# Hybrid encoder, layer 1: one instruction list from the last down projections of layer 0 to the output projection

## The chip, the cores and the metric

The kernel runs on one core of a Trainium2 chip. TensorE does the matmuls, VectorE and ScalarE the elementwise work, GpSimd some elementwise work, and SyncE (SP) issues the DMAs. The metric is the device time of one execution in microseconds; below 0.2% two versions are not told apart here.

## What is computed

A two-layer encoder over two sequences (16 meta tokens and 256 tokens; 16 and 512), with shared weights and in float32. Layer 0 has latent attention, layer 1 windowed attention with a sink per head; both have a squared-ReLU MLP, and the norm stands behind each addition.

```python
for i in range(DEPTH):
    mix = mla_mixer(h, ...) if i % 2 == 0 else gqa_mixer(h, ...)
    h = layer_norm(DN_ALPHA * h + mix, ln1_g[i], ln1_b[i])
    h = layer_norm(DN_ALPHA * h + sqrelu_mlp(h, mlp_w1[i], mlp_w2[i]), ln2_g[i], ln2_b[i])

def gqa_mixer(x, cos, sin, w_qkv, sink, w_o):     # layer 1
    q, k, v = split(x @ w_qkv)                     # 16 query heads, 4 key/value heads of 64
    q, k = partial_rope(q), partial_rope(k)        # the first 16 columns of a head turn
    # a block of 128 queries sees the 16 meta keys and the keys within 128 positions
    s = where(mask, q k^T / 8, -1e30);  m = max(max(s), sink)
    p = exp(s - m) / (sum(exp(s - m)) + exp(sink - m))
    return (p v) @ w_o
```

## The kernel before

Activations lie with the 1024 features on partitions (8 blocks of 128) and the 800 tokens in two halves of 400 columns (`hf` 0 and 1). A product in float32 is made of three matmuls of split operands (`mm3`, L417): high times high, high times low, low times high. So each operand is made as a pair: a cast on ScalarE gives the high part, a subtraction on VectorE the low part (`split`, L434; for weights L297 and L298 in `Weights.load`, which also issues the DMA on SP; three raw and three split buffers, `wraw` and `wsp`).

The two MLPs (`mlp_middle`, L1001) are written as a list of tasks for a `Plan` (L97). A task names its engine, a cost, what it reads and writes, and the buffers it holds. `Plan.order` lays the tasks out in time by these costs, with TensorE's tasks in the order in which they were written, and a buffer free again when the last task that holds it is done (`left`). `Plan.issue` writes all engines' instructions in that order, under `tc.manual_schedule`. The MLP's list ends with the splits of three down weights for the stage after it (`ahead`, L1508 to L1513).

Everything between the two lists is left to the scheduler of the tile framework, which orders each engine's instructions by its own estimate, with hints (`tc.high_priority`, `tc.issue_after`, `after`):

- the last group of down projections of layer 0 (`down0`, L1529), first half, then second, each followed by a layer norm (`ln_fm`, L459): a matmul for the mean, subtractions, squares, sums, a matmul for the sums, square root and reciprocal, a matmul to spread it, then per block a multiplication on VectorE, a scaling on ScalarE (L481) and the split;
- the query, key and value projections (`qk_chunk`, L1601, with the rotation on VectorE and GpSimd; values from L1632). `half_first` (L968) starts with the first half of six chunks and loads three weights twice;
- the attention: 24 items, four pairs of query chunks (`cp`) times six blocks (`b`). `scores1` (L1669) makes two sets of six score matmuls, two row halves of the array at a time, 272 columns wide (400 in blocks 3 and 4), with the masked maximum on VectorE (L1688). `soft` does the exponentials on ScalarE, `norm` the scaling on VectorE and GpSimd (L1725, L1727). `av1` (L1732) transposes the probabilities (L1747 meta, L1756) and multiplies by the values (L1765, L1770). The pieces of five neighbouring items are issued in turns by `GQA_ORDER` (L52), transposes three items behind their scores;
- the output projection (L1809 to L1824), first half, layer norm, second half. Then layer 1's `mlp_middle` begins; its sixth matmul is followed by the mean of the second half (L1147).

PSUM is divided anew for each of these stages (`psum_phase`).

Of the kernel before, what the change touches and what calls it, by code (L numbers as in the profile page):

```python
# [46 lines left out]
QN = 3  # L47
QKV_FIRST = [("q", c) for c in range(2, 2 + QN)] + [("q", 0), ("q", 1), ("k", 0)] + [("q", c) for c in range(2, 2 + QN)]
QKV_REST = [("k", 1)] + [("q", c) for c in range(2 + QN, 8)] + [("v", 0), ("v", 1)]


GQA_ORDER = [("s", 0, 0), ("a", 0, 3), ("a", 1, 3), ("s", 3, 1), ("a", -1, 4), ("s", 1, 0), ("a", 2, 3), ("a", 3, 3), ("s", 2, 0)]  # L52

GQA_LOADS = (4, 5, 6)
GQA_LAG = max(lag for _, _, lag in GQA_ORDER)

# [5 lines left out]


FILL = (None, "pm", "pm", "st", "rb", "rb")
DOWN_FILL = (None, "pm", "pm", "pm", "pm", "pm", "st", "rb")
DOWN_ADD = (None, None, "va", "va", "va", "va", "va", "va")
DOWN_LOAD = ("va", "va", "rc")
# [22 lines left out]
class Held:  # L90


    def __init__(self, tag, make, t=None):
        self.tag, self.make, self.t, self.left, self.fresh = tag, make, t, 0, True


class Plan:  # L97
# [5 lines left out]

    def __init__(self, bufs, own):
# [11 lines left out]
    def task(self, engine, cost, run, reads=(), writes=(), new=(), port=False):  # L116
# [143 lines left out]
    def issue(self):  # L260
        order = self.order()
        tiles = {tag: [make(k) for k in range(self.bufs[tag] - len(self.given[tag]))] for tag, make in self.own.items()}
        for i in order:
            _, _, run, _, held, _ = self.tasks[i]
            for h in held:
                if h.t is None:
                    if h.tag in self.own:
                        k = self.at[id(h)]
                        h.t = tiles[h.tag][k] if isinstance(k, int) else k
                    else:  # L270
                        h.t = h.make()
            run()


class Weights:
# [9 lines left out]
    def load(self, parts=1):  # L285
# [20 lines left out]
        return True  # L306

# [22 lines left out]
def tile_encoder(ctx: ExitStack, tc: tile.TileContext, ins: dict, y):  # L330
# [72 lines left out]
    for layer in range(2):  # L403
        w1 = ins[f"w1_{layer}"]
        if layer == 1:
            for e in QKV_FIRST + QKV_REST:
                use(e, ins["w_" + e[0]][e[1]])
            for _ in range(2):
                for o in range(8):
                    use(("o1", o), ins["w_o1"][o])  # L410
        for j in UP_FIRST[:2]:
            use(("up", j), w1[j])
        for i in range(4):
# [1585 lines left out]
```

## Time and profile before

| | us |
|---|---|
| median of three runs | 1839.02 (1835.86 to 1839.11) |
| the profiled execution | 1837.13 |
| its span | 1835.3 |
| TensorE busy in the span | 1789.3 (97%) |
| VectorE, ScalarE, GpSimd busy | 1351.6, 1011.4, 783.9 |

The span runs from the first instruction to the last on the slowest engine. A matmul's time in the profile includes its way through the array and overlaps the next one, so durations are no measure of TensorE's speed; from start to start is. A busy TensorE can still be slow. The granted clock is given as a share of 2.4 GHz; its two levels are 1.0 and 0.5.

### The profile page before, as it was taken

To read this page: it belongs to the slowest core of one execution; us is meant where nothing else is said; L and a number is where in the kernel's file an instruction comes from. 1 tells how busy PE (TensorE), PEld (TensorE's weight loads), DVE (VectorE), ACT (ScalarE), POOL (GpSimd) and SP (SyncE) were. 2 spreads that over 40 slices of the span, in tenths; PEclk is the share of its full clock that TensorE was granted. 3 is DMA by queue.
4 is the path that set the end of the run, shared out by engine and by line. 5 is a ranking of instruction groups with operands and counts; after the bars stand their busy time and mean duration, and the time that the engine had idled before them with its cause. 6 is when DMAs were issued, how large, how long until landed. Compare 5 with 4: busy or idle time off the path is not lost.

```text
span 1835.3 us, 28950 instructions
## 1 busy us (share of the span) xinstructions
PE 1789.3 (97%) x10808; PEld 1645.0 (90%) x10808; DVE 1351.6 (74%) x2552; ACT 1011.4 (55%) x2146; POOL 783.9 (43%) x616
## 2 busy tenths in 40 slices
PE   9989999999999999999999999999999999999997
PEld 9989889979999999999999997569989889888896
DVE  5478778775876887788776867774875887778767
ACT  5357766773655445544553526782674455545642
POOL 0046655662245445545522232331333566456623
PEclk9999999999999999999999999999999999999999
DMA  5110001104311211222131221002211211222122
GB/s 194 47 41 31 18 21 33 38 29 140 109 58 47 82 59 61 76 71 68 58 122 58 70 73 54 2 1 88 97 63 64 71 67 49 92 69 69 47 92 92
DMA packets 37868, 120.12 MB, mean 65 GB/s; under 512 B 4576, under 2 KB 8800, under 8 KB 37600
## 3 DMA queue, kind: packets, MB, share of 16 engines
q1 hardware_dynamic: 37728, 118.28, 19.3%
q8 instruction: 85, 1.39, 0.3%
q14 instruction: 55, 0.45, 0.1%
HBM read 115.12 MB, written 3.15 MB: 64 GB/s over the span
## 4 chain that ended last, share of the span: by engine, by line
PE 70%; DVE 19%; ACT 6%; issue 3%; POOL 2%; DMA 1%; DVEq 0%; ACTq 0%; POOLq 0%; SPq 0%
PE w L418 14%; PE w L420 14%; PE w L419 14%; PE o L420 2%; PE o L419 2%; PE o L418 2%; PE s L1680 2%; DVE wsp0d L1064 2%; DVE wsp L298 2%; DVE h L1106 2%; PE in L418 1%; PE in L419 1%; PE in L420 1%; PE gav L1765 1%; DVE acc L1371 1%
## 5 line engine op out<-in xcount | busy, mean ns | idle before, releaser
L721 POOL TENSOR_SCALAR p<-p,rs 106x512 f32<-106x512 f32 (+3 forms) x128 | 184.4, 1450 | 134.8 <-DVE pk L720 63.7
L1371 DVE TENSOR_TENSOR acc<-acc,w 128x400 f32<-128x400 f32 (+1 forms) x306 | 176.9, 616 | 21.1 <-PE w L420 18.8
L1106 DVE TENSOR_TENSOR h<-sq,h 128x384 fp32r<-128x384 f32 (+1 forms) x165 | 142.7, 880 | 26.7 <-ACT h L1104 26.6
L297 ACT CAST wsp<-wraw 128x1024 fp32r<-128x1024 f32 (+2 forms) x85 | 78.2, 928 | 78.5 <-PE o L420 62.1
L298 DVE TENSOR_TENSOR wsp<-wraw,wsp 128x1024 fp32r<-128x1024 f32 (+2 forms) x85 | 102.0, 1206 | 21.3 <-ACT wsp L297 20.9
L418 PE MATMUL w<-h,wsp0d 128*128 128x400 f32 x336 | 116.2, 346 | 1.1 <-DVE acc L1371 1.0
L420 PE MATMUL w<-h,wsp0d 128*128 128x400 f32 x336 | 115.7, 344 | 0.3 <-DVE wsp0d L1064 0.3
L419 PE MATMUL w<-h,wsp0d 128*128 128x400 f32 x336 | 116.0, 345 | 0.0
L418 PE MATMUL w<-wsp1d,h 128*128 128x512 f32 x252 | 100.0, 397 | 5.6 <-DVE acc L1371 5.6
L1112 POOL TENSOR_TENSOR sq<-sq,sq 128x400 f32<-128x400 f32 (+1 forms) x56 | 75.1, 1342 | 70.2 <-DVE h L1106 58.1
L420 PE MATMUL w<-wsp1d,h 128*128 128x512 f32 x252 | 100.2, 398 | 0.3
L419 PE MATMUL w<-wsp1d,h 128*128 128x512 f32 x252 | 99.7, 396 | 0.0
L1104 ACT CAST h<-sq 128x384 fp32r<-128x384 f32 (+1 forms) x165 | 84.3, 518 | 26.2 <-POOL sq L1112 24.4
L419 PE MATMUL o<-o,wsp 128*128 128x400 f32 (+1 forms) x256 | 87.9, 343 | 1.3 <-DVE o L435 1.3
L420 PE MATMUL o<-o,wsp 128*128 128x400 f32 (+1 forms) x256 | 87.9, 343 | 1.4 <-DVE wsp L298 1.4
L418 PE MATMUL o<-o,wsp 128*128 128x400 f32 (+1 forms) x256 | 88.8, 347 | 0.3 <-ACT o L435 0.3
L1077 POOL TENSOR_TENSOR wraw0d<-wraw0d,wraw0d 128x512 f32<-128x512 f32 x48 | 69.8, 1472 | 41.2 <-DMA wraw0d<-in_w2b_dram 29.3
L745 ACT ACTIVATE p<-s,nm,rq 106x528 f32<-106x528 f32 (+1 forms) x80 | 63.4, 794 | 41.0 <-DVE nm L744 32.3
L1285 DVE TENSOR_TENSOR sq<-sq,w 128x400 f32<-128x400 f32 (+1 forms) x69 | 38.6, 560 | 52.9 <-PE w L420 52.7
L1058 ACT CAST wsp0d<-wraw0d 128x1024 fp32r<-128x1024 f32 x42 | 43.2, 1050 | 57.6 <-POOL wraw0d L1077 46.1
L743 DVE TENSOR_REDUCE nm<-s 106x1 f32<-106x528 f32 (+1 forms) x80 | 55.8, 700 | 18.3 <-PE s L420 17.4
L1064 DVE TENSOR_TENSOR wsp0d<-wraw0d,wsp0d 128x1024 fp32r<-128x1024 f32 x42 | 63.5, 1512 | 7.1 <-ACT wsp0d L1058 7.1
(1379 smaller groups left out, 6275.7 us busy)
## 6 DMA issues: line engine op xcount, KB each, us to landing
wraw<-in_w_o_dram SPq DMA_DIRECT2D x32, 512.0 KB, 3.3
wraw0d<-in_w2b_dram SPq DMA_DIRECT2D x24, 512.0 KB, 3.2
wraw1d<-in_w2b_dram SPq DMA_DIRECT2D x18, 512.0 KB, 4.0
wraw<-in_w_q_dram SPq DMA_DIRECT2D x11, 512.0 KB, 3.6
wraw<-in_w_in_dram SPq DMA_DIRECT2D x6, 512.0 KB, 4.1
wraw<-in_w_qn_dram SPq DMA_DIRECT2D x8, 384.0 KB, 3.0
wx1d<-in_w2b_dram SPq DMA_DIRECT2D x6, 512.0 KB, 3.2
out_dram<-acc SPq DMA_DIRECT2D x12, 256.0 KB, 2.0
```

What stands on the lines that cost most here:

```text
L297: nc.scalar.copy(sp[:, 0, a:b], raw[:, a:b])
L298: nc.vector.tensor_tensor(sp[:, 1, a:b], raw[:, a:b], sp.bitcast(F32)[:, 0, a:b], ALU.subtract)
L418: nc.tensor.matmul(out, lh, rh, start=start, stop=False, **kw)
L419: nc.tensor.matmul(out, lh, rl, start=False, stop=False, **kw)
L420: nc.tensor.matmul(out, ll, rh, start=False, stop=stop, **kw)
L721: G.tensor_scalar(pt[:qm, META:T], pt[:qm, META:T], rs[:qm, h : h + 1], None, ALU.mult)
L1064: lambda: V.tensor_tensor(dst.t[:, 1, dc], src.t[:, sc], dst.t.bitcast(F32)[:, 0, dc], ALU.subtract),
L1077: lambda x=x, y=y, z=z: G.tensor_tensor(x[0].t[:, x[1]], y[0].t[:, y[1]], z[0].t[:, z[1]], op),
L1104: plan.task("ACT", 530, lambda: S.copy(d.t[:, 0], c.t[:, :n]), reads=[c], writes=[(d, "hi")], new=[d])
L1106: "DVE", 570, lambda: V.tensor_tensor(d.t[:, 1], c.t[:, :n], d.t.bitcast(F32)[:, 0], ALU.subtract),
L1112: plan.task("POOL", 185 + 1.67 * n, lambda: G.tensor_tensor(out.t[:, :n], x.t[:, :n], y.t[:, :n], op), reads=[x, y], writes=[out])
L1371: f = lambda: V.tensor_tensor(z, z, ps.t[:, : z.shape[-1]], ALU.add)
```

## The change

The part between the two MLPs becomes a third `Plan`, `attention1`, with its own list of tasks and TensorE's order written out: the eight down projections of the first half, eight of the second with the first half's norm between them; then query chunks 0 and 1, values, and the other chunks of the first half; chunks 4 to 7 and both key chunks for both halves; then the attention by blocks (blocks 0 to 2 of all pairs, block 5, blocks 3 and 4), with steps of two blocks of k of other projections (`fill`) put between scores, transposes and outputs: the second half of the values and of chunks 0 to 3, and, when blocks 0 to 2 are through, the first half of the output projection. Six weights are loaded twice (four query chunks, two of values). A set of six scores, the transposes of four tiles and a block's value products are one task each. The attention's output takes the place of the queries. `stage` is a task-less buffer that opens memory pools when the tasks that use the old ones are done. `issue(behind)` puts the first instruction of a list on each engine behind the last one of the list before. PSUM stays one ring of eight banks. In `mlp_middle` the three down weights made ahead count as held to the end (`w.left += 1`).

The core of the diff (the bodies of the norm, of the softmax and of the output projection do the same operations as before):

```diff
+FIRST_Q = 4
+ITEMS = [(cp, b) for b in range(3) for cp in range(4)] + [(cp, 5) for cp in range(4)] + [(cp, b) for cp in range(4) for b in (3, 4)]
+BEHIND_T, BEHIND_A = 2, 1
+BESIDE = (3000, 2000, 2000, 1600, 2200, 2200, 2200)
...
+    def stage(self, tag, make):
+        h = Held(tag, make)
+        self.bufs[tag] = 1
+        self.given[tag], self.turns[tag] = [], [h]
+        h.after = set()
+        return h
...
+            deps.update(h.after)
+        for h in ends:
+            h.after.add(n)
...
+            f = getattr(run(), "ins", None)
+            if f is not None:
+                if behind is not None and e in first:
+                    behind(f, first.pop(e))
+                last[e] = f
...
             ahead.append(w)
+            w.left += 1
-            plan.issue()
+            plan.issue(after if l else None)
...
-    psum_phase(w=6, l=2)
-    W.places["last"] = W.places[None]
...
+        plan = Plan(
+            {"wsp": 3, "wraw": 3, "wh": 1, "w": 8, "sqb": 6, "ssb": 1, "ssc": 1, "sqc": 6, "rt": 2, "sh": 1, "sma": 4, "smb": 3, "pta": 2, "ptb": 2,
+             "rm": 4, "nm": 4, "rs": 4, "es": 4, "pk": 4, "ptm": 2, "mask": 1},
...
+        plan.busy = {"DVE": 700.0, "ACT": 700.0, "POOL": 300.0}
+        DVE, ACT, POOL = lambda n: 150 + 1.05 * n, lambda n: 170 + 0.835 * n, lambda n: 185 + 1.67 * n
+        MM = {400: 183, 384: 174, 256: 119}
+        both = lambda *names: [(x, y) for x in names for y in ("hi", "lo")]
+        st1 = plan.stage("projections", open_projections)
+        st2 = plan.stage("attention", open_attention)
+        st3 = plan.stage("wide", open_wide)
+        st4 = plan.stage("norm", open_norm)
...
+        def down(hf, o, between=None):
+            w, ps, a0 = wd[o // 2], new("w"), o % 2 * P
+            def run():
+                for k in range(4):
+                    t, a = tiles[LAST + k][hf], k * 256 + a0
+                    mm3(ps.t[:, :HALF], w.t[:, 0, a : a + P], w.t[:, 1, a : a + P], t[:, 0], t[:, 1], k == 0, k == 3)
+            plan.task("PE", 12 * MM[HALF], run, reads=[w, *both(w)], writes=[ps], new=[ps], ends=[st1])
+            z = acc[:, hf]
+            plan.task("DVE", DVE(HALF), lambda: V.tensor_tensor(z[:, o], z[:, o], ps.t[:, :HALF], ALU.add), reads=[ps], writes=[("acc", hf, o)])
...
+        mean0, sums0, scale0 = layer_norm("b0", 0, acc[:, 0], HALF, 2, 3, lambda: ssb[0].t, out_b(0), "H", "sqb", [ssb[0]], [st2])
+        mean1, sums1, scale1 = layer_norm("b1", 1, acc[:, 1], HALF, 2, 3, lambda: ssb[1].t, out_b(1), "H", "sqb", [ssb[1]], [st2])
...
+            def step(ks):
+                def run():
+                    for k in ks:
+                        a = k * P
+                        mm3(ps.t[:, :n], w.t[:, 0, a : a + P], w.t[:, 1, a : a + P], H[hf][0][:, k, c0:], H[hf][1][:, k, c0:], k == 0, k == 7)
+                plan.task("PE", 6 * MM[n], run, reads=[w, *both(w, *[("H", hf, k) for k in ks])], writes=[ps], new=[ps] if ks[0] == 0 else [], ends=end)
+                if ks[-1] < 7:
...
+                def run(ci=ci, ps=ps):
+                    Q, K = at["Q"][cp], at["K"]
+                    for x, (i, j) in enumerate(((0, 0), (0, 1), (1, 0))):
+                        for gi in range(2):
+                            rows = slice(64 * gi, 64 * gi + 64)
+                            nc.tensor.matmul(ps[gi].t[:, :w], Q[rows, i, ci, q0 : q0 + P], K[j][rows, gp2, k0 : k0 + w], start=x == 0, stop=x == 2)
+                reads = both(("q", 2 * cp + ci, hf), *[("k", gp2, x) for x in kh])
+                plan.task("PE", 3 * (120 if w == 272 else 181) + 100 * (1 - ci), run, reads=[st1, *reads], writes=ps, new=ps, ends=[st4])
...
+        after0 = {0: mean0, 4: sums0, 6: scale0}
+        for o in range(8):
+            down(0, o)
+        for o in range(8):
+            down(1, o)
+            if o in after0:
+                after0[o]()
+        for c in range(2):
+            w = wq(c)
+            for i, f in enumerate(rope("q", c, 0, w)):
+                f()
+                if (c, i) == (0, 3):
+                    mean1()
+        wv = [weights(ins["w_v"][i], f"v{i}") for i in range(2)]
+        for f in values(0, wv):
+            f()
+        for c in range(2, 8):
+            w = wq(c)
+            for i, f in enumerate(rope("q", c, 0, w)):
+                f()
+                if (c, i) == (2, 0):
+                    sums1()
+                if (c, i) == (2, 2):
+                    scale1()
+            if c >= FIRST_Q:
+                for f in rope("q", c, 1, w):
+                    f()
+        for c in range(2):
+            w = weights(ins["w_k"][c], f"k{c}")
+            for hf in range(2):
+                for f in rope("k", c, hf, w):
+                    f()
+        plan.task("SP", 3700, lambda: nc.sync.dma_start(mask.t, ins["mask"][:, MASK_OFF[1] :]), reads=[st2], writes=[mask], new=[mask])
...
+        def fill():
+            wv = [weights(ins["w_v"][i], f"v{i}b") for i in range(2)]
+            for f in values(1, wv):
+                yield 24 * MM[256], f
+            for c in range(FIRST_Q):
+                w = wq(c, "b")
+                for f in rope("q", c, 1, w):
+                    yield 6 * MM[HALF], f
+            yield 0, None
+            for o in range(8):
+                w = weights(ins["w_o1"][o], f"o0{o}")
+                for f in project(0, o, w):
+                    yield 6 * MM[NH], f
...
+        def some(upto):
+            nonlocal done, through
+            while done < upto and not (through and n < 12 + behind):
+                cost, f = next(steps)
+                done += cost
+                if f is None:
+                    through = True
                 else:
+                    f()
+        for n in range(len(ITEMS) + behind):
+            if n < len(ITEMS):
+                cp, b = ITEMS[n]
+                while not {("q", 2 * cp + i, b // 3) for i in range(2)} <= made:
+                    some(done + 1)
+                soft[n] = scores(*ITEMS[n])
+            time += BESIDE[min(n // 4, len(BESIDE) - 1)]
+            some(time - BESIDE[0] / 2)
+            if 0 <= n - BEHIND_T < len(ITEMS):
+                turned[n - BEHIND_T] = transposes(*ITEMS[n - BEHIND_T], *soft.pop(n - BEHIND_T))
+            some(time)
+            if n == 12 + behind - 1:
+                time = done
+            if 0 <= n - behind < len(ITEMS):
+                outputs(*ITEMS[n - behind], *turned.pop(n - behind))
+        for _, f in steps:
+            f()
+        mean2, sums2, scale2 = layer_norm("c0", 0, acc[:, 0, :, META:], NH, 4, 5, lambda: ssc.t[:, :NH], lambda o: (at["h"][0][:, 0, o], at["h"][1][:, 0, o]), ...
+        after1 = {(0, 3): mean2, (2, 2): sums2, (3, 0): scale2}
         for o in range(8):
+            w = weights(ins["w_o1"][o], f"o1{o}")
+            for i, f in enumerate(project(1, o, w)):
+                f()
+                if (o, i) in after1:
+                    after1[o, i]()
+        ahead = [weights(ins["w1_1"][j], f"up{j}") for j in UP_FIRST[:2]]
+        for w in ahead:
+            w.left += 1
+        with tc.manual_schedule(engines={mybir.EngineType.PE, mybir.EngineType.DVE, mybir.EngineType.Activation, mybir.EngineType.Pool, mybir.EngineType.SP}):
+            plan.issue(after)
```

## Rows read from the trace of the kernel before

**Rows 1.** The page: its span, TensorE's busy time, one row of its DMA issues.

```profile
span 1835.3 us, 28950 instructions
...
PE 1789.3 (97%) x10808; PEld 1645.0 (90%) x10808; DVE 1351.6 (74%) x2552; ACT 1011.4 (55%) x2146; POOL 783.9 (43%) x616
...
wraw<-in_w_q_dram SPq DMA_DIRECT2D x11, 512.0 KB, 3.6
```

**Rows 2.** Sums by stretch; columns: stretch, length, busy time of each engine, granted clock, DMA.

```profile
1001.40:1020.90 19.50, 18.16 (x91) 16.59 (x89) 17.03 (x34) 13.12 (x25) 3.19 (x3) 0.91 0.09 28
1120.80:1246.65 125.85, 122.71 (x882) 75.03 (x881) 96.29 (x387) 101.47 (x331) 37.64 (x53) 0.99 0.06 20
1246.65:1317.50 70.85, 70.85 (x406) 70.58 (x405) 45.29 (x58) 28.81 (x40) 17.26 (x13) 1.00 0.32 105
1317.50:1330.60 13.10, 10.84 (x51) 9.89 (x51) 12.28 (x22) 7.73 (x15) 2.19 (x3) 0.87 0.21 80
```

**Rows 3.** TensorE in order of time, end of layer 0's MLP: start, us, what, idle before.

```profile
956.63 0.34 PE L418 MATMUL w<-h,wsp_30z 128*128 128x400 f32 x1
...
958.65 0.34 PE L420 MATMUL w<-h,wsp_30z 128*128 128x400 f32 x1
961.87 0.46 PE L418 MATMUL w<-h,w 128*128 128x400 f32 x1 [2.88 <-DVE sq L1285]
...
965.38 0.54 PE L418 MATMUL dn<-h,wsp0c 128*128 128x400 f32 x1
```

**Rows 4.** VectorE in order of time, at the same place.

```profile
960.11 1.23 DVE L1064 TENSOR_TENSOR wsp0c<-wraw0c,wsp0c 128x1024 fp32r<-128x1024 f32 x1 [0.97 <-ACT wsp0c L1058]
961.25 0.56 DVE L1285 TENSOR_TENSOR sq<-sq,w 128x400 f32<-128x400 f32 x1
```

**Rows 5.** ScalarE in order of time, first layer norm: scalings of two neighbouring blocks.

```profile
1004.81 0.72 ACT L481 ACTIVATE acc<-acc,gb 128x400 f32<-128x400 f32 x1
...
1005.99 0.72 ACT L481 ACTIVATE acc<-acc,gb 128x400 f32<-128x400 f32 x1
```

**Rows 6.** TensorE in order of time, attention: whole pieces, and broken sets of scores.

```profile
1169.41 1.01 PE L1680 MATMUL s<-k,q 64*128 64x272 f32 x12
1170.36 1.08 PE L1765 MATMUL gav<-pt,v 128*64 128x256 f32 x8
...
1186.27 0.45 PE L1680 MATMUL s<-k,q 64*128 64x400 f32 x1
1186.65 1.08 PE L1765 MATMUL gav<-pt,v 128*64 128x256 f32 x6
...
1189.04 0.81 PE L1680 MATMUL s<-k,q 64*128 64x400 f32 x5
1189.78 0.66 PE L1756 MATMUL gt<-ident,sm 128*128 128x128 f32 x4
...
1240.03 1.09 PE L1756 MATMUL gt<-ident,sm 128*128 128x128 f32 x8
1240.96 0.38 PE L1747 MATMUL gm<-ident,pk 128*64 128x128 f32 x2
1241.18 0.60 PE L1756 MATMUL gt<-ident,sm 128*128 128x128 f32 x4
1241.71 1.51 PE L1765 MATMUL gav<-pt,v 128*64 128x256 f32 x12
1243.15 0.65 PE L1770 MATMUL gav<-ptm,vm 64*64 64x256 f32 x4
1243.73 0.66 PE L1756 MATMUL gt<-ident,sm 128*128 128x128 f32 x4
```

**Rows 7.** TensorE and VectorE in order of time, first mean of layer 1's MLP.

```profile
1320.98 1.57 PE L1147 MATMUL w<-sqsum,part 128*128 128x400 f32 x2 [2.26 <-DVE sqsum L1824]
...
1320.28 0.56 DVE L1824 TENSOR_TENSOR sqsum<-sqsum,acc 128x400 f32<-128x400 f32 x1
```

**Rows 8.** VectorE in order of time, attention: a masked maximum behind GpSimd.

```profile
1203.41 0.44 DVE L1688 CUSTOM_DVE_ANT_0 sm<-s,mask 128x272 f32<-128x272 f32 x1 [0.84 <-POOL sm L1725]
```

More of the change, by code (lines that the diff above doesn't have):

```diff
@@ L93, in __init__ @@
     def __init__(self, tag, make, t=None):
[L94 removed]
+        self.tag, self.make, self.t, self.left, self.fresh, self.after = tag, make, t, 0, True, ()
 class Plan:
     LAG = {"PE": 190, "DVE": 70, "ACT": 70, "POOL": 90, "SP": 0}
+    last = {}
     def __init__(self, bufs, own):
@@ L114, in held, with task @@
         return h
-    def task(self, engine, cost, run, reads=(), writes=(), new=(), port=False):
+    def task(self, engine, cost, run, reads=(), writes=(), new=(), port=False, ends=()):
         n, deps, held = len(self.tasks), set(), {}
@@ L258, in order, with issue @@
         return sorted(self.begin, key=lambda i: self.begin[i])
-    def issue(self):
+    def issue(self, behind=None):
         order = self.order()
-        tiles = {tag: [make(k) for k in range(self.bufs[tag] - len(self.given[tag]))] for tag, make in self.own.items()}
+        first, last = Plan.last, {}
+        tiles = {}
         for i in order:
-            _, _, run, _, held, _ = self.tasks[i]
+            e, _, run, _, held, _ = self.tasks[i]
             for h in held:
@@ L306, in load, with give @@
         return True
+    def give(self, key, sp):
+        assert self.specs[self.next][0] == key
+        self.ready[key] = (self.next, sp)
+        self.next += 1
     def get(self, key, ahead=None, keep=False):
@@ L405, in tile_encoder @@
         if layer == 1:
[L406 to L413, printed above, removed]
-            use(("dn", 7, i), ins[f"w2c_{layer}"][i], where="held" if i == 3 else "last")
+            for j in UP_FIRST[:2]:
+                use(("up", j), None, where="given")
+            for i in range(4):
+                use(("dn", 7, i), ins["w2c_1"][i], where="held" if i == 3 else "last")
+        else:
+            for j in UP_FIRST[:2]:
+                use(("up", j), w1[j])
+            for i in range(3):
+                use(("dn", 7, i), None, where="given")
     W = Weights(nc, wp, specs, 3, 3, 2)
@@ new lines, in open_attention, with open_wide, open_norm @@
+    def open_attention():
+        right[2].close()
+        right[1].close()
+        at["c"] = pool("apc", stack=common)
+        at["a"] = pool("apa", stack=first)
+        return at
+    def open_wide():
+        right[0].close()
+        at["b"] = pool("apb", stack=second, side="right")
+        return at
+    def open_norm():
+        for x in (second, first, common, sub):
+            x.close()
+        h1p = pool("h1p", stack=h1s, side="right")
+        at["h"] = [h1p.tile([P, 2, 8, NH], F32R, tag=f"hc{i}", name=f"hc{i}") for i in range(2)]
+        sqp = at["sqp"] = pool("sqp1", stack=h1s, side="right")
+        at["late"] = sq_tile(sqp, "sum1")
+        at["lnc"] = pool("lnc", stack=sub)
+        return at
@@ L1828, in tile_encoder @@
+    psum_phase(w=8)
+    attention1()
+    sub.close()
     l1.close()
+    h, sqp, late_sum = at["h"], at["sqp"], at["late"]
     mlp = ExitStack()
```

610 lines of the change are left out of this document (310 added, 300 removed).

## The prediction

> **What bounds the kernel now.** I read the page first, then the sums by stretch, then the order of time on TensorE where the sums leave a loss. The page says that TensorE is busy in 97% of the span [rows 1], so only two things can be won: the 3% in which it stands still, and time in which it is busy but slow. The profiled execution took 1837.13 us around a span of 1835.3; the median of the three timed runs, 1839.02, is 1.9 us above it. I sum against the profiled execution and add 1.9 at the end.
>
> The change rewrites the part from the last down projections of layer 0 (about 959 us) to the first projections of layer 1's MLP (about 1330). The unit there is a matmul of 400 columns. Twelve of them run densely from 956.63, the last starting at 958.65: 2.02 us for 11 steps, 0.184 us each [rows 3]; by columns, one of 384 costs about 0.176. Against that unit I look for losses:
>
> - The end of the MLP. TensorE stops behind the matmul of 958.65, is idle 2.88 us, and its next 12 matmuls take 961.87 to 965.38 [rows 3]. From 958.83 to 965.38 that is 6.55 us for 2.2 us of work: 4.3 lost.
> - The first layer norm into the first query projection, 1001.40 to 1020.90 [rows 2]. It holds 12 matmuls of 400, 72 of 384 and the norm's mean, 2.2 + 12.7 + 0.4 = 15.3 us; it takes 19.5. Lost: 4.2, of which 1.3 is idle (19.50 less 18.16), and about 1.75 is clock: a mean of 0.91 means that TensorE had 1.2 GHz instead of 2.4 for 18% of the stretch, 3.5 us.
> - The attention, 125.85 us. TensorE is idle for only 3.1 us of it, and yet its weight loads are busy for 75 us, where the output projection next to it has 70.58 of 70.85 [rows 2]. It is busy but not dense; the next part shows why.
> - The output projections, 70.85 us: busy throughout [rows 2], nothing to win.
> - The start of layer 1's MLP, 13.10 us for 48 matmuls of 384 and a mean, 8.8 us: 4.3 lost, of which 2.26 is idle and 1.7 is clock (0.87 of 13.1) [rows 2, 7].
>
> **The change part by part.** *The tail of the MLP: minus 4.3.* The last product waits for an add on VectorE (961.25) that stands behind the split of a down weight (960.11), which itself waited 0.97 us for its cast [rows 4]. The add does not need that weight. The reason is in the code: the Plan believes that a weight tile made for later is free again when its split is done, so it lists the splits of the next two as if their buffers were free early; the chip has to wait until TensorE has let go of them. The new line `w.left += 1` keeps the tile in the Plan's book. The split then goes behind the add, and TensorE finds its operand. Bounds: 0 (the new order puts something else ahead of the add) to minus 4.3. I take all of it, because the row names the one instruction in between.
>
> *Layer norm into the first projection: plus 4.* Before, the scheduler interleaves three query chunks by k, so each normalized block of columns is used three times when it comes. The new list runs chunk 0 alone, in steps of two blocks, and TensorE's order is fixed. ScalarE delivers a block each 1.18 us (its two scalings of 1004.81 and 1005.99) [rows 5]. The first step waits 1.18 longer for its second block; the three others wait 2 x 1.18 less 6 x 0.176 each, 1.3, together 3.9. With the 1.3 of idle that is there today and the 1.75 of clock this is 8.2 lost, against 4.2. Behind TensorE's wait stands the whole rest of the list. Bounds: minus 1 (an earlier start of the chain) to plus 8 (a second spell at 1.2 GHz, and the norm's sums, which come one projection, 2.2 us, sooner behind its mean).
>
> *Attention's own work: minus 20.* What a block costs when its pieces run undivided is in the rows [rows 6]: two sets of scores of 272 columns 0.95 (1169.41 to 1170.36), so about 1.40 for 400 columns; eight transposes 0.93, four 0.53, the meta transposes 0.22, the twelve value matmuls of three key blocks 1.44 (0.96 for two), the meta values 0.58. A block of 272 then is 0.95 + 0.93 + 0.22 + 0.96 + 0.58 = 3.64, one of 400 is 1.40 + 1.46 + 0.22 + 1.44 + 0.58 = 5.10; 16 and 8 of them are 99.0. Today they take 125.85, because sets are broken up: one score, then values, then the other five. The first costs 0.38 (1186.27 to 1186.65), the five 0.74 (1189.04 to 1189.78) [rows 6], together 1.12 for a set that undivided is 0.70. 15 runs of one and 18 of five stand in the stretch. The new list makes a set of scores, a block's transposes and its values one task each, so they stay together. But with projections between them each block has more changes of kind. A broken set has two breaks and costs 0.42 more, about 0.2 a break; I charge 7 us, some 1.3 breaks for each of the 27 places. That leaves 106. Bounds: minus 10 to minus 27.
>
> For this there is a rule. The rows show that a break costs about 0.2 us [rows 6]. The Trainium skill (TensorEngine Tiling (Array Packing), Overview, Key Properties) says that changing the tiling mode drains TensorE. The trace agrees, and the rule speaks against this change, which puts full-array projections between half-array scores and values; what it would make of the time is the third rival.
>
> *New waits in the attention: plus 6.5.* The second half of V (96 matmuls of 256 columns), the second half of four query chunks (96 of 400) and the first half of the output projection (192 of 384) move beside the attention: by columns 11.3 + 17.7 + 33.8 = 62.8 us of TensorE. On average the other engines can follow: today VectorE has 96.3 and ScalarE 101.5 us of work in 125.85 [rows 2]; with 14 weights to split at 1.23 [rows 4] and some 24 rotations and adds at 0.56 VectorE gets about 127 in some 170 us, and ScalarE has only casts added. But three places (12 to 14 of 27) have nothing beside them, and the order is fixed. Today's idle is 0.13 us a block; I take twice that for 27 places, 6.5. Bounds: 0 to 1 us a place, 27.
>
> *The start of layer 1's MLP: minus 3.8.* Today the mean waits for a sum that VectorE ends at 1320.84, 3.3 us behind the last projection, with VectorE busy for 12.28 of the stretch's 13.10: the first half's norm and weight splits stand before it [rows 2, 7]. The new list begins that norm more than a chunk earlier and ends with this sum. It still needs one add and one sum (0.56 each [rows 7]) behind the last matmul, under a cover of six matmuls, 1.06: about 0.5 stays. Bounds: 0 to minus 4.3.
>
> *At nothing:* six weights are loaded twice instead of three. Three more transfers of 512 KB at 3.6 us on SP's queue [rows 1] and three casts and splits lie beside projections that run 4.2 us a weight; without that cover each would cost its 3.6 us. The mask's transfer stands on SP's queue behind the first-half projections and is not read until the fifth block, over 15 us later. The rotation tables come as four transfers instead of two, under the down projections. PSUM is one ring of eight banks instead of two of four; I see no row that prices it.
>
> The sum: -4.3 + 4.0 - 20 + 6.5 - 3.8 = -17.6, so 1819.5 on the profiled execution and **1821 us** on the median. The bounds summed give 1802 to 1864.
>
> **The rivals.** *Second: VectorE becomes the bound beside the projections, 1833.* Places 4 to 11 carry 2 us of projection for 3.64 of attention, and VectorE has about 4.0 + 1.45 us there. What could tip it is GpSimd: a masked maximum came 0.84 us late behind GpSimd's scaling [rows 8]. At 0.7 us instead of 0.25 for each of 27 places the time is 12 us longer. Against it: the mean load of 75%. The Trainium skill (GPSIMD Engine Reference, Specifications) says that GpSimd's SBUF interfaces are shared with VectorE; by that rule the rotations' GpSimd steps, moved in here, lengthen VectorE's work too. [...]
>
> *Third: changes of kind cost more, 1830.* If each place has three more breaks at 0.2, that is 16 us instead of 7.
>
> *Fourth, on the other side: the fixed order makes TensorE wait at the transposes, 1847.* In the list a block's transposes come two blocks behind its scores, today three; where no projection lies between, two blocks are 7.3 us for maximum, exponentials, sums and scaling. If this chain is late, nothing may overtake it. At 1.2 us a place the change loses 26 of its gain. It decides from 0.9 us a place (0.25 + 17.6 / 27). For it: a wait of 1.3 us at the first query projection came with a spell at 1.2 GHz [rows 2]. Against it: the chain's engines are not full.
>
> *Fifth: it does not do what it says, 1835:* the sets stay broken up, or the waits eat them, and only the ends of the stage are won.
>
> **How the numbers follow.** Forecast 0.55, second 0.15, third 0.10, fourth 0.14, fifth 0.06. About 0.2%, 3.7 us, is what a measurement of this kernel can tell from no change: 1835.3 to 1842.7. Faster: nearly all of the forecast and the third, two thirds of the second, a third of the fifth, 0.74. Slower: the fourth and a little of the forecast's upper bound, 0.14. Within: 0.12. The range of 8 in 10 reaches from half-way to the lower bound, 1807, to 1841, which leaves out most of the fourth.
>
> **What would show it.** In the new profile: no idle of 2.9 us at the last product of layer 0's MLP; TensorE waiting in four steps at the first query chunk, some 6 us; scores always in runs of 6 or 12; from the first score to the last output projection some 212 us, today's 196.7 with 29 us of V and query projections moved in; under 1 us at layer 1's first mean. The prediction is wrong if TensorE is idle in that stage for more than 25 us, or if the undivided runs are as long as the broken ones.

## The result and the profile after

The changed kernel takes **1814.5 us** (median; 1810.2 to 1815.7) beside 1839.1 for the kernel before: a ratio of 0.9865, interval 0.9845 to 0.9886. A second comparison gave 0.9877 (0.9863 to 0.9890). The forecast was 1821. The profiled execution took 1813.73 us around a span of 1811.9, 23.4 less than before [rows 1]; 1.0 us more had gone by in it before the change begins (the matmul of 958.65 [rows 3] starts at 959.69).

The page of the changed kernel, its span and TensorE's row, and then the sums by stretch (stretch, length, busy time of each engine, granted clock, DMA):

```profile
span 1811.9 us, 28961 instructions
...
PE 1769.5 (98%) x10808; PEld 1635.5 (90%) x10808; DVE 1344.1 (74%) x2553; ACT 1013.8 (56%) x2141; POOL 784.9 (43%) x617
```

```profile
997.76:1019.61 21.85, 17.05 (x65) 13.46 (x64) 17.11 (x33) 12.35 (x23) 4.20 (x5) 0.77 0.15 50
1093.69:1252.59 158.90, 157.54 (x1224) 121.11 (x1224) 119.30 (x428) 118.60 (x345) 50.22 (x62) 1.00 0.13 41
1252.59:1297.18 44.59, 44.59 (x254) 44.33 (x254) 34.01 (x51) 23.55 (x37) 9.46 (x8) 1.00 0.34 112
1297.18:1306.87 9.69, 9.38 (x51) 8.61 (x50) 8.83 (x16) 5.98 (x11) 2.11 (x2) 1.00 0.22 85
```

As many matmuls as before, 10808, with 20 us less of busy time on TensorE: most of the gain is time in which it was busy but slow. The second stretch is the attention with the work moved beside it: 158.9 us, of which V and the query chunks (96 of 256 columns, 96 of 400) and 151 output matmuls are 55.6 at the dense rate, so 103.3 are the attention's, against 125.85 [rows 2]. TensorE idles 1.4 us in it. The first stretch went the other way: 21.85 us for 11 us of work, at a clock of 0.77.

One place of the attention in the changed kernel, TensorE in order of time (of the projection's six matmuls the first and the last):

```profile
1109.39 1.02 PE L1804 MATMUL wb<-k,q 64*128 64x272 f32 x12
1110.35 0.41 PE L1876 MATMUL wb<-ident,pk 128*64 128x128 f32 x2
1110.59 1.04 PE L1886 MATMUL wb<-ident,sma 128*128 128x128 f32 x8
1111.38 0.43 PE L441 MATMUL wb<-hb,wspq0b 128*128 128x400 f32 x1
...
1112.38 0.34 PE L443 MATMUL wb<-hb,wspq0b 128*128 128x400 f32 x1
1112.65 1.08 PE L1904 MATMUL wb<-pta,v 128*64 128x256 f32 x8
1113.67 0.65 PE L1909 MATMUL wb<-ptm,vm 64*64 64x256 f32 x4
```

Each start to the next: 12 scores 0.96, meta transposes 0.24, eight transposes 0.79, six projections 1.27, values 1.02, meta values 0.57; no wait. Before, the same work stood in runs of one, four, five and six [rows 6].

The start of the layer, TensorE again. This is where time is lost (the rows with idle time, and the matmuls around the fall of the clock):

```profile
1000.43 0.44 PE L441 MATMUL wb<-hb,wspq 128*128 128x384 f32 x1 [0.24 <-ACT hb L1606]
1001.05 0.45 PE L442 MATMUL wb<-hb,wspq 128*128 128x384 f32 x1 [0.18 <-DVE hb L1608]
...
1002.51 0.44 PE L441 MATMUL wb<-hb,wspq 128*128 128x384 f32 x1 [0.31 <-ACT hb L1606]
...
1004.59 0.44 PE L441 MATMUL wb<-hb,wspq 128*128 128x384 f32 x1 [0.33 <-ACT hb L1606]
...
1006.67 0.44 PE L441 MATMUL wb<-hb,wspq 128*128 128x384 f32 x1 [0.33 <-ACT hb L1606]
1007.28 0.59 PE L442 MATMUL wb<-hb,wspq 128*128 128x384 f32 x1 [0.17 <-DVE hb L1608]
1007.67 0.52 PE L443 MATMUL wb<-hb,wspq 128*128 128x384 f32 x1
...
1012.05 1.70 PE L1634 MATMUL wb<-ssb,part 128*128 128x400 f32 x2 [2.90 <-DVE ssb L1696]
```

These are four steps of six matmuls; a step takes 2.08 us where six dense matmuls take 1.06. Then the records go from 0.34 to 0.52, the clock is at its lower level (1.2 GHz) from 1007.4 to 1017.7, and the second half's mean waits 2.90 us for a sum of VectorE. The length of that spell is partly chance: eight more traces of kernels with the same start of the layer show it 3.4 or 6.8 us long, and the time from the first query matmul to the first value matmul between 17.4 and 18.6 us, where it is 19.2 here.

### The profile page after: what moved, and what is told of

Its sections match the earlier page's. It is cut to its first block, busy times and chain, and to the rows that moved or that the text cites. A ratio compares the mean times of both kernels' runs of the same rounds, so it can differ in the third digit from the quotient of the medians.

```text
span 1811.9 us, 28961 instructions
## 1 busy us (share of the span) xinstructions
PE 1769.5 (98%) x10808; PEld 1635.5 (90%) x10808; DVE 1344.1 (74%) x2553; ACT 1013.8 (56%) x2141; POOL 784.9 (43%) x617
## 4 chain that ended last, share of the span: by engine, by line
PE 75%; DVE 16%; ACT 5%; issue 2%; POOL 1%; DMA 1%; DVEq 0%; SPq 0%; ACTq 0%; POOLq 0%
PE w L441 14%; PE w L442 14%; PE w L443 14%; PE wb L441 4%; PE wb L442 4%; PE wb L443 4%; DVE h L1099 2%; DVE wsp0d L1057 2%; PE wb L1904 1%; PE in L441 1%; PE in L442 1%; PE in L443 1%; DVE acc L1364 1%; PE wb L1804 1%; PE wb L1886 1%
## 5 line engine op out<-in xcount | busy, mean ns | idle before, releaser
L1097 ACT CAST h<-sq 128x384 fp32r<-128x384 f32 (+1 forms) x165 | 84.6, 519 | 25.6 <-POOL sq L1105 23.9
L1070 POOL TENSOR_TENSOR wraw1d<-wraw1d,wraw1d 128x512 f32<-128x512 f32 x36 | 53.3, 1498 | 31.8 <-DMA wraw1d<-in_w2b_dram 14.4
L315 DVE TENSOR_TENSOR wsp<-wraw,wsp 128x1024 fp32r<-128x1024 f32 (+2 forms) x52 | 55.5, 1076 | 15.1 <-ACT wsp L314 14.8
L441 PE MATMUL s<-k,q 128*106 128x264 f32 (+5 forms) x208 | 62.3, 300 | 4.3 <-ACT p L776 3.2
L441 PEld LDWEIGHTS w<-h,wsp0d 128*128 128x128 f32 x336 | 63.1, 188 | 3.0 <-DVE acc L1364 2.8
L441 PEld LDWEIGHTS w<-wsp1d,h 128*128 128x128 f32 x252 | 47.3, 188 | 18.4 <-ACT wsp1d L1051 8.0
```

The source lines that it names most:

```text
L441: nc.tensor.matmul(out, lh, rh, start=start, stop=False, **kw)
L1070: lambda x=x, y=y, z=z: G.tensor_tensor(x[0].t[:, x[1]], y[0].t[:, y[1]], z[0].t[:, z[1]], op),
L1097: plan.task("ACT", 530, lambda: S.copy(d.t[:, 0], c.t[:, :n]), reads=[c], writes=[(d, "hi")], new=[d])
```

## The experiments

Ratios are to the kernel before, run on the same chip beside each; the changed kernel's is 0.9865 or 0.9877. One thousandth is 1.8 us.

**One line alone, and all but that line.** To the kernel before (first) it is added, from the changed kernel (second) it is taken:

```
         for w in ahead:          # mlp_middle, layer 0
+            w.left += 1
```

> The kernel before with one line added: the weights fetched ahead for the first up projections of layer 0's MLP get one more reader each in the count that decides when their buffers come free (w.left += 1). Nothing else of the change is in it. Theory (term A of the sum): the 2.88 us idle of TensorE at the last product of that MLP, and the idle around it, come from this count alone. Then the idle is gone, the next matmuls start about 4 us earlier, and the time falls by 4 us, about 1835 where the kernel before has 1839. Rival: the gap has another owner (the square on VectorE itself), only the wait moves to the next weight, and the time falls by less than 1 us.

> The changed kernel without that one line. Theory: the idle of 2.9 us at layer 0's last MLP product is back and the time is 4 us longer, about 1818.5 where the changed kernel has 1814.5. Rival: the new list starts its first weights and down projections by itself, so that the line is not needed in it: within 1 us of the changed kernel.

The weights in question are the three down weights made ahead, not weights of up projections.

Measured: 1831.6 us alone, ratio 0.9969 (0.9959 to 0.9980), 5.0 us between the medians (3.7 to 7.5 by the interval); without it 1817.4, ratio 0.9895 (0.9880 to 0.9910), 3 to 5.5 us more than the changed kernel; these intervals overlap, so there it is the trace that decides. The first row is of the kernel without the line, the others are of the kernel before with it (TensorE, the last product of layer 0's MLP and the first down projection):

```profile
960.85 0.45 PE L441 MATMUL w<-h,w 128*128 128x400 f32 x1 [2.87 <-DVE sq L1278]
```

```profile
962.21 0.34 PE L418 MATMUL w<-h,w 128*128 128x400 f32 x1
...
964.39 0.34 PE L418 MATMUL dn<-h,wsp0c 128*128 128x400 f32 x1
```

Without the line the idle of [rows 3] is back; with it those 12 matmuls take 2.18 us, dense, and nothing waits. The term belongs to that line, in either kernel.

**Sets of scores broken up again.** The same instructions at the same lag; only the order of the pieces on TensorE differs:

```
-  task("PE", run six scores) ...   then: meta transposes, transposes, transposes
+  for each of a block's two sets:
+      task("PE", run six[:1]);  next piece of the transposes
+      task("PE", run six[1:]);  next piece
```

> The changed kernel with each set of six scores issued as one and five, and the pieces of the transposes of two blocks earlier put between them: the same instructions, the same lag, only the order in which kinds alternate, as in the kernel before. Theory 1 (a change of kind costs TensorE about 0.2 us, a broken set 0.42): some 48 sets, so 20 to 28 us more, about 1834 to 1842, with TensorE busy, not idle, for the difference. Theory 2 (the broken runs of before were long because they waited for data): the sets are short again when nothing waits, so 0 to 5 us more, 1814 to 1820.

Measured: 1840.0 us, ratio 1.0019 (1.0010 to 1.0028): the whole gain is gone. One block of it in order of time, and the sums of its attention:

```profile
1138.23 0.39 PE L1806 MATMUL wb<-k,q 64*128 64x272 f32 x1
1138.55 0.41 PE L1886 MATMUL wb<-ident,pk 128*64 128x128 f32 x2
1138.88 0.64 PE L1806 MATMUL wb<-k,q 64*128 64x272 f32 x5
1139.45 0.66 PE L1897 MATMUL wb<-ident,sma 128*128 128x128 f32 x4
1140.04 0.39 PE L1806 MATMUL wb<-k,q 64*128 64x272 f32 x1
1140.36 0.66 PE L1897 MATMUL wb<-ident,sma 128*128 128x128 f32 x4
1140.94 0.64 PE L1806 MATMUL wb<-k,q 64*128 64x272 f32 x5
```

```profile
1094.33:1279.65 185.32, 185.13 (x1224) 128.10 (x1224) 126.05 (x428) 120.67 (x345) 45.34 (x62) 1.00 0.11 35
```

One score takes 0.32, five take 0.57: a set costs 0.89 where undivided it is 0.48, so 0.41 more for its scores; four transposes take 0.59 where eight take 0.79. The stretch is 26.4 us longer; 44 of the 48 sets are cut, so with the share of the transposes a cut set costs 0.60. TensorE is busy for 185.13 of 185.32, and VectorE and ScalarE have the same counts of instructions. Short waits, hidden under the matmul before, are not the cause either: 27 of the 28 single scores of 272 columns take between 0.316 and 0.321 us, and waits for data would differ from place to place. That is theory 1.

**What a break costs.** Twelve undivided scores of 272 columns take 0.96 us, 79 ns each; at a projection's 183 ns for 400 columns one would take 124. In the trace the two scores of a pair, on the two row halves, start 3 to 4 ns apart, and pairs follow each other at 0.12 us (the second of a run at 0.23): two run beside each other in the time of one. A set cut into one and five parts a pair. This kernel cuts into two and four (`six[:2]`, `six[2:]`), with as many changes of kind:

> The kernel with broken sets again, but each set of six scores is issued as two and four instead of one and five, with the same pieces of the transposes between. It tells two causes of the 26 us of broken sets apart. In an undivided run a score of 272 columns comes every 79 ns, though a projection takes 183 ns for 400 columns, 124 for 272: two scores on the array's two row halves run beside each other, and a set issued as one and five leaves one score without its partner. Theory 1 (a change of kind itself costs; the number of changes is the same): within 3 us of the kernel broken as one and five, ratio to the kernel before 1.000 to 1.002. Theory 2 (the lost partner costs, a change costs little): most of the scores' 19 us come back, and with them 12 to 19 us: ratio 0.991 to 0.995.

Again one block in order of time (its first set and the pieces around), and the sums:

```profile
1141.93 0.39 PE L1806 MATMUL wb<-k,q 64*128 64x272 f32 x2
1142.25 0.41 PE L1886 MATMUL wb<-ident,pk 128*64 128x128 f32 x2
1142.59 0.52 PE L1806 MATMUL wb<-k,q 64*128 64x272 f32 x4
1143.04 0.66 PE L1897 MATMUL wb<-ident,sma 128*128 128x128 f32 x4
```

```profile
1092.21:1271.50 179.29, 178.99 (x1225) 121.90 (x1225) 126.22 (x428) 120.49 (x345) 45.30 (x62) 1.00 0.11 36
```

Measured: 1832.6 us, ratio 0.9977 (0.9969 to 0.9986), between the two theories and nearer the first. Two scores take 0.32, four 0.45: 0.77 a set. Of the 0.41 that breaking costs the scores, 0.12 is the lost partner; 0.29 is left with the changes of kind. To this comes what the transposes and meta transposes pay. The stretch gives the whole price: it is 20.4 us longer than in the changed kernel, where one and five gave 26.4; over 44 cut sets with two more changes of kind each that is 0.23 us a change, and 6.0 us in all for the partner. The Trainium skill (TensorEngine Tiling (Array Packing), Tiling Modes, Key Properties) says both, that tiles run in parallel and that a change of mode drains; for scores and transposes these runs agree and give each its price.

**No projections beside the attention**, and **none beside its second part.** In the first, V, the four query chunks and the output projection stand in one piece ahead of or behind the attention; in the second only the output projection does:

```
-BESIDE = (3000, 2000, 2000, 1600, 2200, 2200, 2200)
+BESIDE = (0, 0, 0, 0, 0, 0, 0)
+while not through: some(done + 1)      # before the first block
```

```
-while done < upto and not (through and n < 12 + behind):
+while done < upto and not through:
```

> The changed kernel with no projection beside the attention: the second half of V and of four query chunks is issued in one piece ahead of it, the first half of the output projection in one piece behind it. The blocks' pieces stay undivided and in the same order and lag. Theory 1 (undivided pieces are the gain): 16 blocks of 272 columns at 3.64 and 8 of 400 at 5.10 are 99.0, the attention takes 99 to 105 us of TensorE's work, and the three places that have nothing beside them already now showed idle of 0.25 to 0.49 us, so 24 to 27 places add 6 to 13: about 1820 to 1827. Theory 2 (cover is the gain: the projections hide the softmax, and without them TensorE waits at each block's transposes, the fourth rival's mechanism): 1 us or more a place, 25 us or more idle in the stretch, about 1840 or above.

> The changed kernel with the first half of the output projection in one piece behind the attention, and V and the query chunks beside it as they are. Nothing stands beside the blocks from the thirteenth on. Theory (packing makes most of the gain, cover the rest): these 12 to 15 places wait 0.3 to 0.6 us each, as the three bare places of the changed kernel do, 4 to 8 us: about 1818 to 1822 at a kernel before of 1839. Rival (the lag of two is enough by itself once the list has settled): under 2 us of idle, 1814 to 1816.

The first gives other values for part of the second sequence's output. No instruction of TensorE, VectorE, ScalarE or GpSimd is left out, so the time can be read; but which dependency its order breaks is not known, and a wait that a right order would need may be missing. Measured: 1824.0 us (ratio 0.9926, 0.9912 to 0.9940) and 1816.0 (0.9885, 0.9872 to 0.9899). Of the first kernel the sums of the attention and its two longest waits, then of the second the sums from the first score to the last block:

```profile
1124.04:1237.90 113.86, 105.77 (x882) 68.71 (x881) 92.25 (x390) 99.36 (x322) 36.93 (x53) 0.99 0.03 11
```

```profile
1129.58 0.41 PE L1876 MATMUL wb<-ident,pk 128*64 128x128 f32 x2 [2.62 <-DVE pk L1845]
1131.14 1.82 PE L1886 MATMUL wb<-ident,sma 128*128 128x128 f32 x8 [1.15 <-DVE sma L1857]
```

```profile
1094.15:1229.27 135.12, 131.81 (x1074) 95.73 (x1074) 105.82 (x416) 110.39 (x339) 42.92 (x57) 1.00 0.09 29
```

These are the same 882 matmuls as in the attention of before, alone as there: 113.86 us instead of 125.85 [rows 2]. So undivided pieces give 12 us with no projection near, as theory 1 said, although TensorE idles 8.1 us there and 3.1 before. They are not as fast as beside projections, though: the pieces take 105.8 us where the changed kernel's take 96.9. The transposes are whole and still take 30.6 (23.9 in the changed kernel): between the fourth and the fifth TensorE often waits, part of it too short to show as idle; they stand directly ahead of the values; and 3.4 us of the stretch ran at 1.2 GHz. With the first blocks covered and the later ones bare, the time is within 2 us of the changed kernel, which these few executions can't tell apart, and the stage is 2.2 us longer. TensorE idles 3.3 us in it, between the theory's 4 to 8 and the rival's less than 2. So once the list runs, a lag of two blocks hides most of the softmax by itself. What the projections cover is above all the start, where the first block has nothing ahead of its transposes (2.62 and 1.15 idle).

**Lag of one** (`BEHIND_T, BEHIND_A = 1, 1`), for the fourth rival:

> The changed kernel with the transposes of a block one block behind its scores instead of two. It prices the fourth rival's mechanism. In the run without projections beside the attention, places of 4.1 us with a lag of two left waits of 0.2 to 0.5 us, so the chain from scores to scaled probabilities is about 8 us. Theory: with a lag of one a place gives it only its own length, 4.1 to 6 us, so TensorE waits 2 to 4 us at each of 24 places, 50 to 95 us: 1865 to 1910. Rival: most of that chain's length is queueing that a tighter list removes, 1 us or less a place: 1815 to 1840.

One place, TensorE in order of time:

```profile
1122.47 0.41 PE L1876 MATMUL wb<-ident,pk 128*64 128x128 f32 x2 [1.24 <-DVE pk L1845]
1123.41 1.31 PE L1886 MATMUL wb<-ident,sma 128*128 128x128 f32 x8 [0.53 <-DVE sma L1857]
```

Measured: 1832.2 us, ratio 0.9976 (0.9964 to 0.9987); the stage is 18.8 us longer, 0.8 a place, of which 10 is idle. The mechanism is real, TensorE waits for the scaled probabilities, but its price is far below my 2 to 4 us and lies in the rival's range: the chain from scores to probabilities is not 8 us long when TensorE asks for it sooner.

**Fewer changes of kind.** The projection in one piece, the meta transposes moved next to the values:

```
-some(time - BESIDE[0] / 2)              # ahead of the transposes
+turned[n - BEHIND_T][3]()               # meta transposes, ahead of outputs()
```

> The changed kernel with two orders changed at each place of the attention: the projection beside it is put in one piece behind the block's transposes instead of in two, and the meta transposes directly ahead of the values (both use half of the array's columns). The kinds in a row go from seven changes to five at a place where both pieces stood, from six to five elsewhere. Theory (a change of kind has a price): two halves of 1.20 and 1.27 us become one of 2.35, 0.12 less, and the meta transposes save up to 0.2: 24 places, 2 to 6 us less, 1809 to 1812.5. Rival: only a change that breaks up a chain of scores or transposes costs, the rest overlaps: within 1 us of 1814.5.

Measured: 1813.9 us, ratio 0.9876 (0.9859 to 0.9892): no gain, as the rival said. The projections in the stage do take 57.2 us instead of 60.3. But eight transposes take 0.85 instead of 0.79, the meta transposes 0.31 instead of 0.24, together 2.9 us in the stage, and idle time and waits within the scores eat 2.6 more: the price moved to the neighbours. The trace shows where it stands: behind the scores and ahead of the values, and whichever piece is there pays it. Between projections, meta transposes and transposes a change costs nothing; the first transpose starts 0.109 us behind the last meta transpose, as one transpose behind another. By the rule of the Trainium skill (TensorEngine Tiling (Array Packing), Tiling Modes, Key Properties) on modes alone, one change fewer a place at the 0.23 us of the broken sets would be an estimate of 5.5 us. The runs do not bear that out: the changes taken away were those that cost nothing.

**The start of the layer.** Two and three query chunks interleaved step by step:

```
-for c in range(2): for f in rope("q", c, 0, wq(c)): f()     # mean1 behind chunk 0
+for fs in zip(*[rope("q", c, 0, wq(c)) for c in range(3)]):  # range(2) in the first run
+    for f in fs: f()
+mean1()
-after0 = {0: mean0, 4: sums0, 6: scale0}
+after0 = {0: mean0, 4: sums0, 5: scale0}                     # three chunks only
```

> The changed kernel with the first two query chunks of the first half interleaved, step by step, and the second half's mean behind both: each normalised block that arrives feeds 12 matmuls instead of 6. Theory (term B went wrong because 24 sparse matmuls could not cover the norm's casts and the mean behind them): TensorE at the first query chunk waits 0.2 us or less a step instead of 0.3 with a low clock, the 2.9 us wait at the second mean is gone, and of the 10.9 us lost there some 7 are won back: about 1807.5 where the changed kernel has 1814.5. Rival: the norm's chain itself is late (VectorE's and ScalarE's sums end when they end), the wait only moves to the first chunk: less than 2 us won.

> The changed kernel with three query chunks interleaved, the first norm's scaling one down projection earlier, and the second half's sums and scaling beside the value projections. Theory as for two chunks, with 18 matmuls a block (3.2 us at 183 ns) against 2.36 us for two casts: no wait of TensorE at all there, no spell at 1.2 GHz, 9 to 10 of the 10.9 us won: about 1805. Rival: the second norm, now with less time behind its mean, makes the second half's projections wait instead: 1810 or above.

Measured: 1810.0 us, ratio 0.9856 (0.9839 to 0.9874), and 1807.3, ratio 0.9839 (0.9821 to 0.9858). TensorE's row of the mean with two chunks, then with three, and the sums over the three chunks:

```profile
1012.61 1.03 PE L1634 MATMUL wb<-ssb,part 128*128 128x400 f32 x2 [3.95 <-DVE ssb L1696]
```

```profile
1010.19 0.94 PE L1634 MATMUL wb<-ssb,part 128*128 128x400 f32 x2 [0.35 <-DVE ssb L1696]
```

```profile
997.07:1010.66 13.59, 13.24 (x76) 12.78 (x75) 8.76 (x17) 8.08 (x13) 1.25 (x1) 1.00 0.10 39
```

With two chunks the steps run on, but the mean waits longer (3.95): VectorE's sum is not there sooner for it. The mean starts 13.06 us behind the first query matmul, where it was 11.62, with 24 more matmuls (4.2 us) in front of it. Between theory and rival, 2 to 4 us of the 7 were won. With three, 72 matmuls and the mean take 13.59 us for 13.1 of work, at a clock of 1.00, as the theory said. The kernel is only 5 to 7 us faster than the changed one all the same, between the theory's 9 to 10 and the rival's 4.5 or less: at the second norm's squares TensorE then waits 0.51 us (1020.44) and runs at 1.2 GHz from 1022.8 to 1026.2.

**All together, beside the changed kernel once more.** Three chunks, the second norm's sums a little later, the fill spread thinner (`BESIDE = (2300, 1800, 1800, 1800, ...)`) and the last short blocks in the order 2, 3, 0, 1:

> The changed kernel with what the runs so far bear out: three query chunks interleaved behind the first norm, its scaling one down projection earlier, the second half's sums behind the value projections and its scaling behind the second step of the fourth chunk; and the projections beside the attention spread thinner over its first 14 places, with the blocks whose query chunks are there already first, so that no place is bare. Theory: the 1 us of waits at the second norm's squares and the 1.2 us at the three bare places go, 2 us below the kernel with three chunks interleaved: ratio to the kernel before about 0.983, 1805 where that has 1836.4. Rival: thinner cover makes waits elsewhere and the second norm's scaling comes late for the half's projections: ratio 0.985 or above.

> The changed kernel itself, beside the others on the same chip: ratio to the kernel before 0.9865, as it was, about 1811.6 where that has 1836.4. It bounds what the kernel with three chunks interleaved gains on it: 4 to 6 us if the gain seen against the kernel before is real, under 2 us if it was the chip.

Measured: 1808.0 us, ratio 0.9836 (0.9822 to 0.9849), beside 1814.3, ratio 0.9877 (0.9863 to 0.9890). Its sums, first query projection and attention, stand below. The two intervals don't touch: this version is **6.4 us faster than the changed kernel**, 29 faster than the one before.

```profile
1002.36:1015.95 13.59, 13.24 (x76) 12.78 (x75) 8.76 (x17) 8.08 (x13) 1.25 (x1) 1.00 0.11 39
1086.34:1246.94 160.60, 158.88 (x1224) 121.46 (x1224) 117.48 (x428) 118.34 (x345) 50.33 (x62) 1.00 0.13 41
```

From the first query projection to the first score it takes 84.0 us, the changed kernel 93.3. The thinner fill gives 2.6 of that back by the last output projection, 1.7 of it in the attention (160.60 against 158.90: scores now wait for query chunks), as its rival said. Against three chunks alone the gain is within the measurement.

## Why the prediction was right, and where it was off

Direction and order of size were right, by these steps (us; the sum stood at -17.6, the span shows -23.4):

| step | forecast | trace | what settles it |
|---|---|---|---|
| end of layer 0's MLP | -4.3 | -4.3 | one line alone: -5.0 |
| first layer norm | +4.0 | +6.7 | three chunks: gone |
| attention's own work | -20 | -24 | broken: +26.4 |
| new waits in it | +6.5 | +1.4 | lag of one: +18.8 |
| start of layer 1's MLP | -3.8 | -3.4 | trace only |

The rest is a wait of 0.7 us in the V projections that the kernel before had, and the 1.0 that this execution was late.

**Attention's own work.** The mechanism was right; the term was too small by 4, of which 1.7 is a spell at 1.2 GHz (1126.5 to 1129.9, among the scores) that the kernel before had in this stage and that is not the pieces' doing. Starts to starts on TensorE, idle taken off, summed by kind over the stage (runs, us):

| kind, matmuls | before | after | broken 1+5 | broken 2+4 |
|---|---|---|---|---|
| scores, 288 | 49, 38.8 | 24, 25.6 | 90, 44.8 | 90, 38.7 |
| transposes, 224 | 50, 30.7 | 24, 23.9 | 52, 30.5 | 52, 30.5 |
| values, 224 | 30, 31.9 | 24, 27.8 | 24, 27.8 | 24, 27.8 |
| meta transposes, 48 | 24, 7.4 | 24, 5.7 | 24, 7.9 | 24, 7.9 |
| meta values, 96 | 24, 14.0 | 24, 13.9 | 24, 13.9 | 24, 13.9 |
| idle | 3.1 | 1.4 | 0.2 | 0.3 |

Undivided the pieces are 96.9, where I had 99.0: eight transposes are 0.79, not the 0.93 of [rows 6], which stood between other kinds. The 7 I charged for changes of kind beside projections are 5.0: the projections take 60.6 for 55.6 of dense work, in 36 runs, 0.14 a run. The third rival had the sign of a cost that exists and a size that doesn't: a projection next to transposes costs nothing, one next to scores or values does. (The stretch of before holds 16 runs of five scores, not 18; no sum rests on it.)

**New waits** was the step furthest off: 6.5 for 1.4. I took twice the idle of before for 27 places, though the rows gave no reason for waits where VectorE would be 75% loaded (it is: 119.3 of 158.9). Idle of note appears in only one of the three bare places, three times:

```profile
1166.25 0.38 PE L1876 MATMUL wb<-ident,pk 128*64 128x128 f32 x2 [0.25 <-DVE nm L1821]
1167.10 0.66 PE L1886 MATMUL wb<-ident,sma 128*128 128x128 f32 x4 [0.47 <-DVE sma L1857]
1168.25 0.66 PE L1886 MATMUL wb<-ident,sma 128*128 128x128 f32 x4 [0.49 <-DVE sma L1857]
```

The expectation of the run without projections took them for three places. The fourth rival needed 0.9 us a place; even with a lag of one it is 0.8, with two 0.06. The second rival fell by the same sums: VectorE is no bound. Its row [rows 8] shows a wait for a result of GpSimd, not a longer instruction of VectorE; and with GpSimd's rotations moved in here VectorE's busy time in the whole span is 1344.1 us, where it was 1351.6 [rows 1].

**First layer norm** was too small by 2.7. The four steps came, at 2.08 us for 1.06. What I had only as a bound happened: the second mean waits 2.90, and the clock is at 1.2 GHz for 10.3 us where before it was 3.4. That length is the longest of the nine traces with this start; in the shortest of them the miss is 0.9, not 2.7. The cause was as written: before, each normalised block served three chunks. With three chunks again the stretch takes 0.5 us more than its work.

**The ends** were right. At layer 1's first mean 0.31 us of idle is left of 2.26, and no spell at 1.2 GHz follows it:

```profile
1298.70 0.91 PE L1140 MATMUL w<-sqsum,part 128*128 128x400 f32 x2 [0.31 <-DVE sqsum L1942]
```

From the first score to the last output projection it takes 203.5 us where I gave 212: the two misses in the attention, 9 us together. The profiled execution lies 5.8 below its forecast of 1819.5, and that is these 9 less the 2.7 of the first norm, with half a microsecond from the small terms. That the forecast came this close is in part luck: the misses of the attention and of the first norm have opposite signs. The range's lower end is mis-stated too: half-way from 1821 to the lower bound of 1802 is 1811.5, not 1807. The measured 1814.5 lies inside either.

## What to carry over

When TensorE is busy but its weight loads are not, sum its time by kind of instruction and count the runs: one broken set cost 0.60 us here, 0.41 of it in its scores, without a wait anywhere, and 25 more runs of scores in the kernel before went with 11.5 us (13.2 less the spell at 1.2 GHz). Keep the scores together and in pairs; changes among projections and transposes cost nothing here. With whole pieces and projections in between, a lag of two blocks hides the softmax but for 1.4 us. A list of one's own should keep what the scheduler did well: where a norm feeds the first projection, let each block serve several weights before TensorE goes on.

## What the runs showed of the hardware

- Scores on 64 rows: the two of a pair, on the two row halves, start 3 to 4 ns apart, and pairs of 272 columns follow each other at 0.12 us, the time of one such matmul at a projection's rate (0.124). A cut through a pair costs 0.12 us.
- Cutting sets of scores cost 0.23 us for each change between scores and transposes. A change among projections, transposes and meta transposes costs nothing (0.109 us from the last meta transpose to the first transpose), and the run that took such changes away saved nothing.
- Twice an idle of 2.9 us (before and in the kernel without the one line) was followed by matmuls at 1.2 GHz; but in the changed kernel the clock fell at 1007.4, behind steps in which no single idle was over 0.33 us, and stayed low for 10.3 us; other traces with the same steps show 3.4 and 6.8. With the same work dense, in the last version, the stretch ran at a clock of 1.00.
